# Batch normalisation of 32 x 256 x 128 x 128 floats: two DMA rings, with and without a hold on the stores

## The chip, the cores and the metric

The kernel runs on one core of one Trainium2 chip. The metric is device time in microseconds (us) of one execution; for the kernel before it is the median of three runs. The profile is of one further look at the same program, whose span from the first to the last instruction is a little shorter than the device time of that run (2480.7 us against 2482.53 us).

## The reference

Inference-time batch normalisation in float32: every channel is multiplied by one number and another is added, both worked out from the channel's four parameters.

```python
def reference(x, gamma, beta, running_mean, running_var):
    # x: (32, 256, 128, 128); the others: (256,), reshaped to (1, 256, 1, 1)
    eps = 1e-5
    return gamma * (x - mean) / np.sqrt(var + eps) + beta
```

The input holds 537 MB and the output as much, so the work is nearly all transport: each value is read once, scaled and shifted, and written once.

## The kernel before

A tile is one image and one block of 128 channels: 128 partitions of 16384 floats, 64 KB a partition, 8.39 MB in all. There are 64 tiles and three buffers (`NBUF = 3`), which are used in turn and in place: loaded, computed, stored. SyncE issues all loads, ScalarE all stores, VectorE computes. The semaphores are kept by hand: `loaded[s]` and `stored[s]` count the transfers of buffer `s`, `done` counts VectorE's tiles.

The loads. Tile 0 comes in two parts, so that computing can begin early. A later load waits until its buffer has been stored, and then until the load before it has landed, so that the loads' ring holds one transfer at a time:

```python
nc.sync.dma_start(out=bufs[0][:, left], in_=xr[0][:, left]).then_inc(early, 16)
zeroed = step(nc.vector.memset(rows[:], 0.0))
# ... four small loads of the parameters into rows ...
nc.sync.dma_start(out=bufs[0][:, right], in_=xr[0][:, right]).then_inc(loaded[0], 16)
for i in range(1, NT):
    s, turn = i % NBUF, i // NBUF
    if turn:
        nc.sync.wait_ge(stored[s], 16 * turn)                                  # L99
    inst = nc.sync.dma_start(out=bufs[s][:], in_=xr[i]).then_inc(loaded[s], 16)  # L100
    if i >= 2:
        inst._wait_ge(loaded[(i - 1) % NBUF], 16 * ((i - 1) // NBUF + 1))
```

The early writes. Each of the 16 DMA engines writes 128 bytes of zeros to an output row of tile 0, long before that row is written in earnest:

```python
blanked = step(nc.vector.memset(blank[:], 0.0))
nc.scalar.dma_start(out=outr[0][0 :: P // NE, 0:B], in_=blank[:])._wait_ge(vec, blanked).then_inc(touched, 16)
```

Then the parameters are turned into a scale and a shift per channel (some ten small instructions, left out here), and the tiles follow. A store waits until its tile is computed; ahead of that ScalarE waits until the store before it has landed, so that the stores' ring holds one transfer at a time as well:

```python
def store(i, after):
    s = i % NBUF
    inst = nc.scalar.dma_start(out=outr[i], in_=bufs[s][:]).then_inc(stored[s], 16)   # L143
    inst._wait_ge(done, after)

def turn_of_store(i):
    nc.scalar.wait_ge(stored[(i - 1) % NBUF], 16 * ((i - 1) // NBUF + 1))

compute(0, left)._wait_ge(early, 16)
compute(0, right)._wait_ge(loaded[0], 16)
nc.scalar.wait_ge(touched, 16)
store(0, 2)
for i in range(1, last):
    compute(i)._wait_ge(loaded[i % NBUF], 16 * (i // NBUF + 1))     # L132, on VectorE
    turn_of_store(i)
    store(i, i + 2)
```

`compute` is one VectorE instruction: times `scale_t`, plus `shift_t`. The last tile is shared by VectorE (9216 columns) and ScalarE (7168 columns, L161), and its store waits for both but not for the store before it.

Of the kernel before, what the change touches and what calls it, by code (L numbers as in the profile page):

```python
# [8 lines left out]
NBUF = 3  # L9
# [4 lines left out]
@with_exitstack  # L14
def kernel(
    ctx: ExitStack,
    tc: tile.TileContext,
    x: bass.AP,
    gamma: bass.AP,
    beta: bass.AP,  # L20
    running_mean: bass.AP,
    running_var: bass.AP,
    out: bass.AP,
):
    nc = tc.nc
    eps = 1e-5
    f32 = mybir.dt.float32

    N, C, H, W = x.shape
    P = nc.NUM_PARTITIONS  # L30
    assert C % P == 0
    NCB = C // P
    HW = H * W
    NT = N * NCB
    B = 32
    NQ = P // B
    NE = 16
    NPAR = 4

    xr = x.rearrange("n (cb p) h w -> (n cb) p (h w)", p=P)  # L40
    outr = out.rearrange("n (cb p) h w -> (n cb) p (h w)", p=P)

    params = ctx.enter_context(tc.tile_pool(name="params", bufs=1))
    data = ctx.enter_context(tc.tile_pool(name="data", bufs=1))
    bufs = [data.tile([P, HW], f32, name=f"t{s}", tag=f"t{s}") for s in range(NBUF)]
    rows = params.tile([B, NPAR * C], f32, name="rows", tag="rows")
    turned = params.tile([B, NPAR * C], f32, name="turned", tag="turned")
    par = params.tile([P, NPAR, NCB], f32, name="par", tag="par")
    blank = params.tile([NE, B], f32, name="blank", tag="blank")
    eps_t = params.tile([P, 1], f32, name="eps_t", tag="eps")  # L50
    std_t = params.tile([P, NCB], f32, name="std_t", tag="std")
    rstd_t = params.tile([P, NCB], f32, name="rstd_t", tag="rstd")
    scale_t = params.tile([P, NCB], f32, name="scale_t", tag="scale")
    ms_t = params.tile([P, NCB], f32, name="ms_t", tag="ms")
    shift_t = params.tile([P, NCB], f32, name="shift_t", tag="shift")

    loaded = [tc.alloc_semaphore(f"loaded{s}") for s in range(NBUF)]
    stored = [tc.alloc_semaphore(f"stored{s}") for s in range(NBUF)]  # L60
    touched = tc.alloc_semaphore("touched")
    early = tc.alloc_semaphore("early")
    done = tc.alloc_semaphore("done")
    fetched = tc.alloc_semaphore("fetched")
    vec = tc.alloc_semaphore("vec")
    act = tc.alloc_semaphore("act")

    with tc.tile_critical():  # L68
        count = [0]

        def step(inst, sem=None, value=None):

            if sem is not None:
                inst._wait_ge(sem, value)
            elif count[0]:
                inst._wait_ge(vec, count[0])
            inst.then_inc(vec, 1)
            count[0] += 1
            return count[0]

        left, right = slice(0, HW // 4), slice(HW // 4, HW)
        last = NT - 1

        nc.sync.dma_start(out=bufs[0][:, left], in_=xr[0][:, left]).then_inc(early, 16)
        zeroed = step(nc.vector.memset(rows[:], 0.0))  # L87
        for r, ap in enumerate((running_var, gamma, beta, running_mean)):
            inst = nc.sync.dma_start(out=rows[0:NE, r * C : (r + 1) * C], in_=ap.partition_broadcast(NE))  # L89
            if r == 0:  # L90
                inst._wait_ge(vec, zeroed)
            inst.then_inc(fetched, 16)
# [9 lines that stand above are left out]
                inst._wait_ge(loaded[(i - 1) % NBUF], 16 * ((i - 1) // NBUF + 1))  # L102


        blanked = step(nc.vector.memset(blank[:], 0.0))  # L105
        nc.scalar.dma_start(out=outr[0][0 :: P // NE, 0:B], in_=blank[:])._wait_ge(vec, blanked).then_inc(touched, 16)


        step(nc.vector.memset(eps_t[:], eps))  # L109
        step(nc.vector.transpose(out=turned[:], in_=rows[:]), fetched, 16 * NPAR)  # L110

        blocks = turned.rearrange("p (rc q b) -> p rc q b", q=NQ, b=B)
        flat = par.rearrange("p r cb -> p (r cb)")
        for q in range(NQ):
            placed = step(nc.vector.tensor_copy(out=flat[q * B : (q + 1) * B], in_=blocks[:, :, q, 0]))  # L115
        var_t, gamma_t, beta_t, mean_t = (par[:, r] for r in range(NPAR))
        nc.scalar.activation(  # L117
            out=std_t[:],
            in_=var_t,
            func=mybir.ActivationFunctionType.Sqrt,  # L120
            bias=eps_t[:],
            scale=1.0,
        )._wait_ge(vec, placed).then_inc(act, 1)
        step(nc.vector.reciprocal(out=rstd_t[:], in_=std_t[:]), act, 1)  # L124
        step(nc.vector.tensor_mul(out=scale_t[:], in0=gamma_t, in1=rstd_t[:]))  # L125
        step(nc.vector.tensor_mul(out=ms_t[:], in0=mean_t, in1=scale_t[:]))  # L126
        ready = step(nc.vector.tensor_sub(out=shift_t[:], in0=beta_t, in1=ms_t[:]))  # L127
        nc.vector.wait_ge(vec, ready)

        def compute(i, cols=slice(0, HW)):  # L130
            t, cb = bufs[i % NBUF], i % NCB
            return nc.vector.tensor_scalar(  # L132
                out=t[:, cols],
                in0=t[:, cols],
                scalar1=scale_t[:, cb : cb + 1],
                scalar2=shift_t[:, cb : cb + 1],
                op0=mybir.AluOpType.mult,
                op1=mybir.AluOpType.add,
            ).then_inc(done, 1)

        def store(i, after):
            s = i % NBUF
            inst = nc.scalar.dma_start(out=outr[i], in_=bufs[s][:]).then_inc(stored[s], 16)  # L143
            inst._wait_ge(done, after)

        def turn_of_store(i):
            nc.scalar.wait_ge(stored[(i - 1) % NBUF], 16 * ((i - 1) // NBUF + 1))

        compute(0, left)._wait_ge(early, 16)
        compute(0, right)._wait_ge(loaded[0], 16)  # L150
        nc.scalar.wait_ge(touched, 16)
        store(0, 2)
        for i in range(1, last):
            compute(i)._wait_ge(loaded[i % NBUF], 16 * (i // NBUF + 1))
            turn_of_store(i)
            store(i, i + 2)

        turns = last // NBUF + 1
        compute(last, slice(0, VCOLS))._wait_ge(loaded[last % NBUF], 16 * turns)
        t, cb = bufs[last % NBUF], last % NCB  # L160
        nc.scalar.activation(  # L161
            out=t[:, VCOLS:],
            in_=t[:, VCOLS:],
            func=mybir.ActivationFunctionType.Identity,
            bias=shift_t[:, cb : cb + 1],
            scale=scale_t[:, cb : cb + 1],
        )._wait_ge(loaded[last % NBUF], 16 * turns).then_inc(done, 1)
        store(last, last + 3)

        for s in range(NBUF):  # L170
            nc.sync.wait_ge(stored[s], 16 * ((NT - s + NBUF - 1) // NBUF))
# [30 lines left out]
```

## Time and profile before

| what | value |
|---|---|
| time, median of 3 runs | 2483.66 us (2482.53 to 2484.41) |
| span of the profile | 2480.7 us |
| VectorE busy | 564.1 us, 23% |
| ScalarE busy | 7.9 us |
| bytes by DMA | 1073.84 MB, mean 433 GB/s |
| one tile on VectorE (128x16384) | 8.81 us |
| one load, one store: issue to landing, median | 38.6 us each |

TensorE isn't used. The profile calls the loads' ring q1 and the stores' ring q10. A DMA packet is one contiguous piece that one of the 16 DMA engines moves; here that is a partition's 64 KB. The DMA view gives for each ring its packets, its megabytes and the time that they took as a share of the time of 16 engines in the stretch asked for; packets count where they start, so a share in a short stretch can come out at a little over or under 100%. The waits of SyncE's queue are given by the line of the instruction that waited and by what released it.

### The profile page before, as it was taken

What the parts mean: (1) busy time and instruction counts of PE and PEld (TensorE: products, weight loads), DVE (VectorE), ACT (ScalarE), POOL (GpSimd) and SP (SyncE); (2) the same over time, 40 slices, a digit from 0 to 9 for tenths busy, and PEclk for the clock granted to TensorE, in tenths of its full rate; (3) what the DMA queues carried; (4) which work ended last, traced back from release to release, by engine and by line L of the source; (5) the groups of instructions that cost most, each with busy time, mean ns of one, the idle gap of its engine ahead of it and who ended that gap; (6) DMA issues with size and microseconds to landing.
All of it is one profiled execution on the core that took longest, in us unless ns stands there. A gap on an engine that the chain in (4) does not pass through costs nothing.

```text
span 2480.7 us, 392 instructions
## 1 busy us (share of the span) xinstructions
DVE 564.1 (23%) x77; ACT 7.9 (0%) x3; POOL 0.2 (0%) x4
## 2 busy tenths in 40 slices
DVE  3121221212212122121221222212222122121221
ACT  0000000000000000000000000000000000000001
POOL 0000000000000000000000000000000000000000
DMA  9999999999999999999999999999999999999999
GB/s 415 431 440 433 429 439 435 428 437 439 426 437 440 425 439 439 426 437 438 429 435 437 431 433 437 433 431 437 436 429 436 436 430 434 440 428 434 440 428 406
DMA packets 18739, 1073.84 MB, mean 433 GB/s; under 512 B 2160, under 2 KB 2224, under 8 KB 2224
## 3 DMA queue, kind: packets, MB, share of 16 engines
q1 hardware_dynamic: 9488, 536.94, 50.0%
q10 hardware_dynamic: 9248, 536.88, 49.9%
q14 instruction: 3, 0.02, 0.0%
HBM read 536.94 MB, written 536.87 MB: 433 GB/s over the span
## 4 chain that ended last, share of the span: by engine, by line
DMA 99%; ACT 0%; issue 0%; SPq 0%; DVE 0%; DVEq 0%
DMA t<-in_x_dram 99%; ACT t L161 0%; SPq L89 0%; DVE rows L87 0%; SPq L93 0%; DVE blank L105 0%; DVE eps_t L109 0%; DVEq L197 0%; SPq L68 0%
## 5 line engine op out<-in xcount | busy, mean ns | idle before, releaser
L132 DVE TENSOR_SCALAR t<-t,scale_t,shift_t 128x16384 f32<-128x16384 f32 (+2 forms) x65 | 560.6, 8624 | 1882.4 <-DMA t<-in_x_dram 1882.3
L161 ACT ACTIVATE t<-t,shift_t,scale_t 128x7168 f32<-128x7168 f32 x1 | 6.4, 6361 | 2438.7 <-DMA t<-in_x_dram 2438.7
L110 DVE STREAM_TRANSPOSE turned<-rows 32x1024 f32<-32x1024 f32 x1 | 1.2, 1233 | 7.1 <-DMA rows<-in_running_mean_dram 7.1
L117 ACT ACT_TABLE_LOAD x1 | 1.3, 1283 | 2.7 <-DVE eps_t L109 2.7
L87 DVE MEMSET rows<- 32x1024 f32 x1 | 0.9, 912 | 1.2 <-SPq L68 1.2
L115 DVE COPY par<-turned 32x8 f32<-32x8 f32 x4 | 0.6, 162 | 0.1
L117 ACT ACTIVATE std_t<-par,eps_t 128x2 f32<-128x2 f32 x1 | 0.3, 295 | 7.6 <-DVE par L115 7.6
L124 DVE RECIPROCAL rstd_t<-std_t 128x2 f32<-128x2 f32 x1 | 0.2, 165 | 0.4 <-ACT std_t L117 0.4
L127 DVE TENSOR_TENSOR shift_t<-par,ms_t 128x2 f32<-128x2 f32 x1 | 0.2, 163 | 0.0
L126 DVE TENSOR_TENSOR ms_t<-par,scale_t 128x2 f32<-128x2 f32 x1 | 0.2, 161 | 0.0
L125 DVE TENSOR_TENSOR scale_t<-par,rstd_t 128x2 f32<-128x2 f32 x1 | 0.2, 160 | 0.0
L186 POOL MEMSET const-bfloat16-1.0<- 128x1 bf16 x1 | 0.1, 102 | 0.0
L186 POOL MEMSET const-uint8-127<- 128x1 uint8 x1 | 0.1, 102 | 0.0
L186 POOL MEMSET const-float32-1.0<- 128x1 f32 x1 | 0.1, 99 | 0.0
L105 DVE MEMSET blank<- 16x32 f32 x1 | 0.1, 85 | 0.1
L186 POOL MEMSET const-float32-0.0<- 128x1 f32 x1 | 0.1, 98 | 0.2 <-issue 0.2
L109 DVE MEMSET eps_t<- 128x1 f32 x1 | 0.1, 59 | 0.1
## 6 DMA issues: line engine op xcount, KB each, us to landing
t<-in_x_dram SPq DMA_DIRECT2D x1, 6144.0 KB, 19.4
t<-in_x_dram SPq DMA_DIRECT2D x1, 2048.0 KB, 7.7
out_dram<-t ACTq DMA_DIRECT2D x64, 38.6
t<-in_x_dram SPq DMA_DIRECT2D x63, 38.6
rows<-in_running_var_dram SPq DMA_DIRECT2D x1, 16.0 KB, 6.4
out_dram<-blank ACTq DMA_DIRECT2D x1, 2.0 KB, 5.8
rows<-in_gamma_dram SPq DMA_DIRECT2D x1, 16.0 KB, 6.2
rows<-in_beta_dram SPq DMA_DIRECT2D x1, 16.0 KB, 5.9
```

Source lines behind the costliest of these rows:

```text
L87: zeroed = step(nc.vector.memset(rows[:], 0.0))
L105: blanked = step(nc.vector.memset(blank[:], 0.0))
L110: step(nc.vector.transpose(out=turned[:], in_=rows[:]), fetched, 16 * NPAR)
L115: placed = step(nc.vector.tensor_copy(out=flat[q * B : (q + 1) * B], in_=blocks[:, :, q, 0]))
L117: nc.scalar.activation(out=std_t[:], in_=var_t, func=mybir.ActivationFunctionType.Sqrt, bias=eps_t[:], scale=1.0,)._wait_ge(vec, placed).t ...
L124: step(nc.vector.reciprocal(out=rstd_t[:], in_=std_t[:]), act, 1)
L125: step(nc.vector.tensor_mul(out=scale_t[:], in0=gamma_t, in1=rstd_t[:]))
L126: step(nc.vector.tensor_mul(out=ms_t[:], in0=mean_t, in1=scale_t[:]))
L127: ready = step(nc.vector.tensor_sub(out=shift_t[:], in0=beta_t, in1=ms_t[:]))
L132: return nc.vector.tensor_scalar(out=t[:, cols], in0=t[:, cols], scalar1=scale_t[:, cb : cb + 1], scalar2=shift_t[:, cb : cb + 1], op0=myb ...
L161: nc.scalar.activation(out=t[:, VCOLS:], in_=t[:, VCOLS:], func=mybir.ActivationFunctionType.Identity, bias=shift_t[:, cb : cb + 1], scale ...
L186: nc = _bacc.Bacc("TRN2", target_bir_lowering=False, num_devices=1)
```

## The change

The stores' ring is no longer held to one transfer. ScalarE issues a store as soon as its tile is computed, even while the store before is still under way; the loads' ring alone keeps its hold. The early writes of 128 bytes go too, with their buffer, their memset, their semaphore and the wait for it. The aim is a simpler schedule in which a store that is ready need not wait for another. Loads, buffers, computing and the last tile stay as they were; lines move up, so that L100 and L99 become L98 and L97, L143 becomes L137, and L132 becomes L126.

```diff
--- before.py
+++ after.py
@@ -46,7 +46,6 @@
     rows = params.tile([B, NPAR * C], f32, name="rows", tag="rows")
     turned = params.tile([B, NPAR * C], f32, name="turned", tag="turned")
     par = params.tile([P, NPAR, NCB], f32, name="par", tag="par")
-    blank = params.tile([NE, B], f32, name="blank", tag="blank")
     eps_t = params.tile([P, 1], f32, name="eps_t", tag="eps")
     std_t = params.tile([P, NCB], f32, name="std_t", tag="std")
     rstd_t = params.tile([P, NCB], f32, name="rstd_t", tag="rstd")
@@ -58,7 +57,6 @@
 
     loaded = [tc.alloc_semaphore(f"loaded{s}") for s in range(NBUF)]
     stored = [tc.alloc_semaphore(f"stored{s}") for s in range(NBUF)]
-    touched = tc.alloc_semaphore("touched")
     early = tc.alloc_semaphore("early")
     done = tc.alloc_semaphore("done")
     fetched = tc.alloc_semaphore("fetched")
@@ -102,10 +100,6 @@
                 inst._wait_ge(loaded[(i - 1) % NBUF], 16 * ((i - 1) // NBUF + 1))
 
 
-        blanked = step(nc.vector.memset(blank[:], 0.0))
-        nc.scalar.dma_start(out=outr[0][0 :: P // NE, 0:B], in_=blank[:])._wait_ge(vec, blanked).then_inc(touched, 16)
-
-
         step(nc.vector.memset(eps_t[:], eps))
         step(nc.vector.transpose(out=turned[:], in_=rows[:]), fetched, 16 * NPAR)
 
@@ -143,16 +137,11 @@
             inst = nc.scalar.dma_start(out=outr[i], in_=bufs[s][:]).then_inc(stored[s], 16)
             inst._wait_ge(done, after)
 
-        def turn_of_store(i):
-            nc.scalar.wait_ge(stored[(i - 1) % NBUF], 16 * ((i - 1) // NBUF + 1))
-
         compute(0, left)._wait_ge(early, 16)
         compute(0, right)._wait_ge(loaded[0], 16)
-        nc.scalar.wait_ge(touched, 16)
         store(0, 2)
         for i in range(1, last):
             compute(i)._wait_ge(loaded[i % NBUF], 16 * (i // NBUF + 1))
-            turn_of_store(i)
             store(i, i + 2)
 
         turns = last // NBUF + 1
```

## The prediction

> **What bounds the kernel now.** I read the page's busy times first, then the chain of work that ended last, then the waits of SyncE's DMA queue, then the DMA record cut to short windows. The page gives VectorE 23% of the span and the 16 DMA engines a 9 in every slice. The chain says the same:
>
> ```profile
> DMA 99%; ACT 0%; issue 0%; SPq 0%; DVE 0%; DVEq 0%
> ...
> q1 hardware_dynamic: 9488, 536.94, 50.0%
> q10 hardware_dynamic: 9248, 536.88, 49.9%
> ```
>
> q1 is the ring of the loads (issued by SyncE), q10 the ring of the stores (issued by ScalarE). Their shares of the 16 engines' time add up to 99.9%, so nearly no engine time is unused. One period of the steady part, from one load's issue at 53.02 us to the next at 91.63 us, in the DMA record:
>
> ```profile
> DMA packets 288, 16.78 MB, mean 435 GB/s; under 512 B 32, under 2 KB 32, under 8 KB 32
> q1 hardware_dynamic: 144, 8.39, 50.1%
> q10 hardware_dynamic: 144, 8.39, 50.1%
> ```
>
> Of each ring's 144 packets 128 are rows of 64 KB (a tile has 128 rows of 16384 floats) and 16 are the small ones that count up the semaphore. An engine thus moves 8 + 8 rows in 38.61 us: 2.41 us a row. I call that a slot. A period is 16 slots and holds no empty one.
>
> The two holds are seen in the waits of SyncE's queue:
>
> ```profile
> SPq L100 <- DMA t<-in_x_dram: 1375.3, 62, 48.1
> SPq L99 <- DMA out_dram<-t: 1008.6, 61, 16.7
> ```
>
> L99 ends when the store of three tiles before has landed, 1008.6/61 = 16.5 us after the previous load was issued; L100 ends when the previous load has landed, some 22 us later. So the stores aren't what keeps a load back. L143's issue times agree: ScalarE issues a store about 16.5 to 17 us after the load of its tile landed, though VectorE is done with it after 8.81 us. The remaining 8 us are the wait for the previous store, which the change removes. What do the rings do meanwhile? Cut to the stretch around the end of a load (49.55 to 56.8 us), and around the end of a store (66.4 to 73.7 us), first the one and then the other:
>
> ```profile
> q10 hardware_dynamic: 48, 3.15, 100.1%
> q1 hardware_dynamic: 16, 0.00, 0.1%
> ```
> ```profile
> q1 hardware_dynamic: 48, 3.15, 99.4%
> q10 hardware_dynamic: 16, 0.00, 0.1%
> ```
>
> While the load ring is empty, every engine runs three store rows in a row (48 = 3 x 16) and the load's semaphore packets; while the store ring is empty, three load rows and the store's semaphore packets. Both times the engines are 99 to 100% busy. Elsewhere rows of the two rings alternate. The end of the chain in order of time is the last thing to see:
>
> ```profile
> 2411.84 38.65 DMA t<-in_x_dram
> 2450.50 0.02 issue
> 2450.52 6.36 ACT t L161
> ```
>
> The last load lands at 2450.50, its tile is computed in 6.36 us, and the last store (issued at 2456.91) lands about 22.6 us later, near the end of the span.
>
> **What the Trainium skill says.** "DMA: Bandwidth & Descriptors", section "Queues, rings and completion order", says that a DMA engine takes turns between the rings that have work, a packet at a time. The windows above agree: outside the gaps a load row follows a store row. The same page under "Where 436 GB/s comes from" gives 435.2 GB/s as the ceiling of one core's DMA; this trace moves 434 to 435 in the steady part. Its section "Issuing engines are not separate DMA queues" says that rings of two issuing engines use the same 16 engines and interleave, so that a second ring saves only issue time. The trace agrees: a gap in one ring is filled by the other. That page has nothing on a first write by an engine, which the removed 128-byte writes are for.
>
> **The change part by part.**
>
> (1) The 128-byte writes go, with one memset (85 ns) and ScalarE's wait for them. The page's row for them is
>
> ```profile
> out_dram<-blank ACTq DMA_DIRECT2D x1, 2.0 KB, 5.8
> ```
>
> Issued at 2.30 us they have landed by about 8.1, long before the first store at 30.12, so the wait costs nothing now and its removal gains nothing. Their 2 KB weigh nothing either: 16 packets of 13 ns. What they may do is to take a first-write delay off the first real store. The packet records show that the load row before the first store row is still stretched here, to 2.8 to 3.5 us from 2.41. If more of that comes back without them, I estimate 0 to 1 us (the size of the stretch that is there), on the path, once.
>
> (2) Stores are queued as soon as the tile is computed. In the steady part no slot is empty now, so at most 16 slots a period can stay 16 slots: gain 0 in the 62 periods. What moves is the phase. Call a load's landing T; the next load's first row runs 3.8 us later (landing at 53.0, first row at 56.8). Slot 0 is that row, so T is at slot -1.6. Now the next store is issued at T + 16.5, slot 5.2, and its first row is in slot 7 (73.7 us). After the change it is issued at T + 8.86, slot 2.1; ready some 0.4 slot later (the first load's rows start 1.0 us after its issue) and, as now, one row later than it is ready: slot 4.
>
> At first the stores gain on the loads. When the first store ends (66.4 us), the second is already queued (compute ends at 61.8), so the three load rows in a row become one load row and a store row in turn. The load in flight thereby loses two slots, its landing moves by 2 x 2.41 = 4.8 us, and the store ring comes 8 us forward against it. But a store can't start before its tile is loaded and computed. From there the store ring runs empty ahead of slot 4, and the gap that the hold made is back, made by VectorE's 8.81 us in place of the hold. After one or two periods, going through the slots: loads in 0, 1, 2, 3, 5, 7, 9, 11; stores in 4, 6, 8, 10, 12, 13, 14; the next load in 15, and the eighth store row in the slot after that. The following period needs 17. The average is 16 slots again, 38.6 us. Cost in the steady part: 0.
>
> (3) The end. Store 63 can put its first row on an engine 6.36 us of compute and about 1.0 us of start after the last landing T': T' + 7.4. Now store 62 keeps the engines busy until about T' + 7 to T' + 9 (its semaphore packets run from 2457.4 to 2459.7, and T' is 2450.5), so hardly an engine waits. After the change store 62 is further along: in a period of 15 slots it ends at slot 16, with T' at 13.4, which is T' + 6.2 us; in one of 17 it ends at slot 17 with T' at 15.4: T' + 3.8 us. The 16 engines stand still for 7.4 - 6.2 = 1.2 us or 7.4 - 3.8 = 3.6 us. This is new time, since the bytes are the same.
>
> Sum: 0 to 1 us for (1), 0 for the steady part, 1.2 to 3.6 us for the end: 1.2 to 4.6 us, middle 2.9. I round down to 2.3, because the engines aren't in step (the two groups of semaphore packets at the end are about 1.6 us apart) and stragglers hide part of such a hole: 2483.66 + 2.3 = 2486.0 us.
>
> **The rivals.** (A) The hold is a loss now: the store ring is empty for about 7 us of each period (66.4 to 73.7), and 62 x 7 = 434 us of ring time looks like a prize. Against it: 48 load rows in just that stretch and 99.4% of the engines' time. The change would then be no faster. All that could still be had is the span less the rows: 64 x 2 x 8 rows x 2.418 us (the packet records' duration) = 2476.0 us of the 2480.7, that is 4.7 us, of which 1.9 pass before the first packet and about 1 after the last. At best the change makes 2482.
>
> (B) A second queued store crowds out the load in flight: three store rows to one load row, so that each load takes 2 slots longer, 62 x 4.8 = 298 us, some 2780 us in all. For it: the first such period will do just that. Against it: a store can't run ahead of the load that feeds it, so it can happen in one or two periods only, and the slots given to stores early are missing from their work later.
>
> (C) The hold keeps the 16 engines in step, and without it some run ahead until a load waits for a straggler with empty engines beside it. For it: the groups 1.6 us apart even now, hold and all. Against it: every load still waits for all 16 engines of the one before. If a tenth of a slot were lost per period, 62 x 0.24 = 15 us: 2499 us. I give this about one chance in ten, and half of such cases are small.
>
> **Range and chances.** Low end: nothing at the end and a lucky draw, one or two us under 2483.66: 2482. High end: 4.6 us and a few of (C): 2491. 2% would be 50 us; faster by that is below the rows' 2476 us, and slower needs (B) in every period. Faster 0.003, within 2% 0.99, slower 0.007.
>
> **What would show it.** Right: in the waits of SyncE's queue L98 and L97 (the old L100 and L99) change places in part, the stores having landed about 8 us sooner after each load's issue, so a mean under 12 us in place of 16.5; stores are issued 8.9 us after their load landed; loads take 36 to 41 us in turn with a mean of 38.6; the steady part still has 434 to 435 GB/s; the DMA record has a hole of 1 to 4 us just ahead of the last store. Step (1) is seen in the stretch of rows at 31 to 34 us. Wrong: a steady part under 432 GB/s (then (C)), load periods with a mean above 39 us ((B)), or no hole at the end. If VectorE's 8.81 us per tile became longer beside queued stores, step (2) would also fall.

## The result and the profile after

The changed kernel takes 2506.3 us (2503.28 to 2509.88, 6 runs) against 2483.23 us (6 runs): ratio 1.0089, 95% interval 1.0076 to 1.0102. It is slower by 0.9%, some 23 us, where the prediction had 2486.0 and a range up to 2491.

The span and the rings on the page of the changed kernel:

```profile
span 2504.6 us, 327 instructions
...
q1 hardware_dynamic: 9488, 536.94, 50.4%
q10 hardware_dynamic: 9216, 536.88, 49.5%
```

Multiply the shares by the spans. The loads' ring took 50.0% x 2480.7 = 1240 us of the 16 engines before and 50.4% x 2504.6 = 1262 us after; the stores' ring 49.9% x 2480.7 = 1238 us and 49.5% x 2504.6 = 1240 us. (A share is rounded to 0.1%, so each product is good to 1.2 us.) The shares add up to 99.9% in both. So the DMA engines do not stand idle more; the load packets take 22 us longer for the same bytes, and that is nearly the whole loss of 23.9 us in the span. VectorE is as before, with 564.1 us.

The waits of SyncE's queue:

```profile
SPq L98 <- DMA t<-in_x_dram: 1832.0, 62, 48.2
SPq L97 <- DMA out_dram<-t: 575.1, 61, 16.5
```

On average the store that a load waits for lands 575.1/61 = 9.4 us after the issue of the load before, in place of 16.5: the phase moved forward by 7 us. In the chain in order of time (start, duration, what), loads alternate:

```profile
994.84 37.20 DMA t<-in_x_dram
...
1032.06 41.02 DMA t<-in_x_dram
...
1073.09 36.61 DMA t<-in_x_dram
```

From the load issue at 53.11 us to that at 2435.12 there are 61 periods: 39.05 us each, against 38.67 before (53.00 to 2411.84). The periods account for the loss: 61 x 0.38 = 23 us.

Where in a period? Compare 6.3 us beginning at the issue of a store, which hold the last load rows before the new store's first rows, and these. First the kernel before (1037.55 to 1043.85 us), then the changed one in a short period (1003.7 to 1010.0 us) and in the long one after it (1040.9 to 1047.2 us):

```profile
q1 hardware_dynamic: 26, 1.70, 62.4%
q10 hardware_dynamic: 16, 1.05, 38.4%
```
```profile
q1 hardware_dynamic: 23, 1.51, 63.1%
q10 hardware_dynamic: 15, 0.98, 36.0%
```
```profile
q1 hardware_dynamic: 27, 1.77, 64.8%
q10 hardware_dynamic: 20, 1.05, 38.4%
```

All the load packets here are 64 KB rows, and so are the store packets but for four small semaphore packets in the last window. The mean of a row is the share times 16 engines times 6.3 us, divided by their number: a load row took 0.624 x 100.8 / 26 = 2.42 us before; after the change it took 0.631 x 100.8 / 23 = 2.77 us in the short period and 0.648 x 100.8 / 27 = 2.42 us in the long one. A store row took 2.42 us in all three.

These two periods are a strong and a weak case. The trace has a record of every packet with its start, time and size. Over tiles 3 to 61 the mean of such a window is 2.61 us in short periods and 2.46 us in long ones, and what the load rows of a period take above 2.418 us each adds up to some 0.55 us per engine in a short period and 0.16 us in a long one. Taken over all load rows after 53 us, this excess is 21 us per engine in the changed kernel and 0.5 us before. About 12 of the 21 us sit in load rows that end 9 to 16 us after the load's issue, around the new store's first row; 5 us sit in the rows before those, mostly in a load's first row, and 4 us in the two or three rows after.

### The profile page after: what moved, and what is told of

The parts are those of the page before. It is cut to its first block, busy times and chain, and to the rows that moved or that the text cites. A ratio compares the mean times of both kernels' runs of the same rounds, so it can differ in the third digit from the quotient of the medians.

```text
span 2504.6 us, 327 instructions
## 1 busy us (share of the span) xinstructions
DVE 564.1 (23%) x76; ACT 7.9 (0%) x3; POOL 0.2 (0%) x4
## 3 DMA queue, kind: packets, MB, share of 16 engines
q1 hardware_dynamic: 9488, 536.94, 50.4%
q10 hardware_dynamic: 9216, 536.88, 49.5%
## 4 chain that ended last, share of the span: by engine, by line
DMA 99%; ACT 0%; SPq 0%; issue 0%; DVE 0%; DVEq 0%
DMA t<-in_x_dram 99%; ACT t L150 0%; SPq L87 0%; DVE rows L85 0%; SPq L91 0%; DVE eps_t L103 0%; DVEq L186 0%; SPq L66 0%
## 5 line engine op out<-in xcount | busy, mean ns | idle before, releaser
L126 DVE TENSOR_SCALAR t<-t,scale_t,shift_t 128x16384 f32<-128x16384 f32 (+2 forms) x65 | 560.5, 8624 | 1908.3 <-DMA t<-in_x_dram 1908.2
```

The costliest lines, as they stand in the source:

```text
L126: return nc.vector.tensor_scalar(out=t[:, cols], in0=t[:, cols], scalar1=scale_t[:, cb : cb + 1], scalar2=shift_t[:, cb : cb + 1], op0=myb ...
```

## The experiments

Each kernel ran beside the kernel before on the same chip; ratios are to those runs. Theory P says that what costs is how early in the period the store arrives, W that the missing early writes cost, H that the wait as such keeps the 16 engines in step, I that a ring that stood idle is slow to start. The others are named as they come.

| run | what | store issued after landing of its load | ratio (95%) | us |
|---|---|---|---|---|
| e1 | hold removed, early writes kept | as changed kernel | 1.0094 (1.0077-1.0110) | 2507.5 |
| e2 | hold kept, early writes removed | 16.95 us | 0.9998 (0.9989-1.0007) | 2484.2 |
| f3 | free, computing shared | 6.45 us | 1.0195 (1.0179-1.0210) | 2533.6 |
| changed kernel | free | 8.85 us | 1.0089 (1.0076-1.0102) | 2506.3 |
| e5 | free, 2 dummies | 11.4 us | 1.0043 (1.0028-1.0058) | 2497.2 |
| e6 | free, 4 dummies | 13.9 us | 1.0025 (1.0015-1.0034) | 2493.7 |
| e12 | free, 6 dummies | 16.5 us | 1.0010 (1.0003-1.0017) | 2487.6 |
| e3 | free, 8 dummies | 19.0 us | 1.0009 (1.0000-1.0018) | 2486.4 |
| e7 | free, VectorE delayed | 21.9 us | 1.0012 (1.0005-1.0020) | 2491.0 |
| e8 | free, no computing | as changed kernel | 1.0098 (1.0083-1.0113) | 2511.8 |
| e9 | changed kernel, tiles jump by 32 | as changed kernel | 1.0082 (1.0067-1.0097) | 2504.6 |
| e10 | changed kernel, falling order | as changed kernel | 1.0097 (1.0082-1.0112) | 2508.9 |
| e11 | e2, tiles jump by 32 | as e2 | 1.0002 (0.9993-1.0011) | 2484.2 |
| f1 | both rings free | 8.85 us | 1.0076 (1.0060-1.0092) | 2505.8 |
| f2 | stores held, loads free | see below | 1.2998 (1.2977-1.3020) | 3229.8 |
| e4 | held, 2.5 us pause | see below | 1.0964 (1.0948-1.0981) | 2724.2 |

The kernel before took 2484.59 us beside e1 to e4, 2487.50 beside e5 to e8, 2484.58 beside e9 to e12 and 2485.53 beside f1 to f3.

**Which part of the change? e1 and e2.**

```diff
 e1, from the kernel before:
-            turn_of_store(i)
             store(i, i + 2)
 e2, from the changed kernel:
+            nc.scalar.wait_ge(stored[(i - 1) % NBUF], 16 * ((i - 1) // NBUF + 1))
             store(i, i + 2)
```

> The kernel before with the stores' hold alone removed; the early writes of 128 bytes stay. If the early writes set how the 16 engines stand to one another for the whole run (theory W), this stays near the time before: 2483 to 2487 us. If the free stores are the cause (theories P, H and I below), it is as slow as the changed kernel: 2502 to 2510 us, with loads of 41 and 36.7 us in turn.

> The changed kernel with the stores' hold put back; no early writes. Theory W: about 2500 us or more. All others: the time before, 2481 to 2486 us, with loads of 38.6 us each. What lies between this and the kernel before is the worth of the early writes: I expect 0 to 2 us.

The early writes are worth nothing that can be measured (e2, to 0.1%), and the whole loss comes with the free stores (e1). W falls.

**The wait or the phase? e3 and e4.** In e3 ScalarE is made busy between a tile's computing and its store, with no wait for a store:

```diff
+            if 1 <= i < last:
+                nc.scalar.wait_ge(done, after)
+                for k in range(8):      # each waits for the one before; the last releases the store
+                    nc.scalar.activation(out=rows[:], in_=turned[:], func=Identity, ...)
             inst = nc.scalar.dma_start(out=outr[i], in_=bufs[s][:]).then_inc(stored[s], 16)
```

> The changed kernel (free stores, no early writes), but ScalarE runs eight dummy instructions on a small scratch tile between the end of a tile's computing and the issue of its store (not for the first and last tile). I estimate 8 to 9 us for them, from 6.36 us for 7168 columns, so the store is issued some 17 us after its load landed, as in the kernel before, without any wait for another store. Theory P (what costs is where in the load's 16 slots the store arrives): back to 2482 to 2488 us, all loads near 38.6 us. Theory H (the wait for a landed store keeps the 16 engines in step): stays at 2500 us or more, load rows still stretched.

The eight dummies took 10.15 us, as the timeline of e3 shows (start, duration, engine, line, operation):

```profile
982.60 8.81 DVE L127 TENSOR_SCALAR t<-t,scale_t,shift_t 128x16384 f32<-128x16384 f32 x1 [32.22 <-DMA t<-in_x_dram]
991.45 10.15 ACT L141 ACTIVATE rows<-turned,shift_t,scale_t 32x1024 f32<-32x1024 f32 x8 [30.88 <-DVE t L127]
1001.63 0.34 ACTq L151 DMA_DIRECT2D out_dram<-t  x1
```

The store comes 19.0 us after the landing at 982.6, unheld, and the loss is all but gone. H falls as the cause of the 0.9%: no store waits for another. (What is left, 0.1% here and in e12, isn't explained.) The load rows in the 6.3 us from that store's issue, in e3's DMA record:

```profile
q1 hardware_dynamic: 21, 1.38, 50.6%
```

0.506 x 100.8 / 21 = 2.43 us a load row: not stretched. Yet e3's loads still alternate between 41 and 36.2 us, so the alternation that I predicted is there and costs nothing by itself. And in the short periods, as in this window, the previous store had landed 2.2 us before the new one was issued, with hardly any stretch (0.11 us per engine and period): an idle ring alone isn't enough. In the changed kernel the ring is idle before the store in the short periods too, for 1.6 us, and these have most of the stretch; but f3, below, has the most stretch of these three kernels, and no idle stores' ring. So I falls as the cause, though an idle ring may add to what an early store does; that wasn't tested by itself.

e4 was meant for I alone. It holds the stores and pauses ScalarE (two of the dummies) after the landing of the store before:

```diff
+            nc.scalar.wait_ge(stored[(i - 1) % NBUF], 16 * ((i - 1) // NBUF + 1))
+            # then, as in e3 but with range(2): dummies, then the store
```

> The hold put back, no early writes, and two dummy ScalarE instructions (estimate 2 to 2.3 us) between the landing of the store before and the issue of the next store. The stores' ring is then empty and idle for some 2 us before each store, as the changed kernel has it in every second period (1.97 us). Theory I (a store that meets a ring idle for 2 us stretches the load row before it by about 0.4 us on each engine): 62 x 0.4 = 25 us slower than with the plain hold, near 2508 us. Theories P and H: no more than 0 to 5 us slower than with the plain hold, since phase and step are nearly as before.

No theory foresaw 2724 us, so as a test of I it is inconclusive. A held store that is issued 2.5 us later ends later too, and with the hold this adds up: the stores are issued 19.4, 24.2, 29.4 and 33.9 us after a load's issue in the first four periods. Then loads wait for stores:

```profile
SPq L98 <- DMA out_dram<-t: 2505.6, 61, 50.3
SPq L99 <- DMA t<-in_x_dram: 99.5, 6, 48.0
```

From there both rings run empty together in each period. One such period (1013.47 to 1056.1 us) in e4's DMA record:

```profile
q1 hardware_dynamic: 144, 8.39, 49.4%
q10 hardware_dynamic: 144, 8.39, 45.4%
```

5.2% of the engines' time is unused, and a load row takes 0.494 x 16 x 42.63 / 128 = 2.63 us on the mean. The pause is one that the hold passes on from store to store; it isn't 2.5 us once.

**How much by how much? e5, e6, e12, and f3 on the other side.** e5, e6 and e12 are e3 with `range(2)`, `range(4)` and `range(6)`.

> Free stores, each issued two dummy ScalarE instructions (1.24 us each, measured) after its tile is computed: 11.4 us after its load landed in place of 8.85. If the cost falls off smoothly with the store's place in the load: about 2497 us. If it is a matter of reaching one slot (2.41 us) further: either 2505 or 2487.

> The same with four dummy instructions: the store is issued 13.9 us after the load landed, between the changed kernel (8.85) and the one with eight (19.0). Smooth: about 2490 us. Theory P only asks that it is no slower than with two dummies.

> Free stores, six dummy ScalarE instructions (7.5 us) after each tile's computing: the store is issued 16.4 us after its load landed, within 0.6 us of where the hold puts it (16.9), but waits for no store. Theory P: as the kernel before, ratio 0.999 to 1.002. If the wait as such had a use beyond the phase: 1.003 or more.

The cost falls smoothly. At 16.5 us, where the hold would put it, a free store costs 0.1%. f3 goes the other way and makes computing faster:

```diff
-            compute(i)._wait_ge(loaded[i % NBUF], 16 * (i // NBUF + 1))
+            compute(i, slice(0, VCOLS))._wait_ge(loaded[i % NBUF], 16 * (i // NBUF + 1))
+            # ScalarE: the other 7168 columns, counted on a semaphore of its own
             store(i, i + 2)
```

> The changed kernel with every tile shared by VectorE (9216 columns) and ScalarE (7168 columns, 6.36 us), so that a store is issued about 6.5 us after its load landed in place of 8.85: faster computing. Theory P: slower than the changed kernel, on the line of 1.0025 at 13.9 us, 1.0043 at 11.4 and 1.009 at 8.85: about 1.014, 2515 to 2530 us, with more stretched load rows. If the effect levels off: 2500 to 2510 us. If it was bound to a store at about one slot's place: under 2500 us.

A tile is ready 2.4 us sooner, and the kernel is slower by another 1.1%, more than a straight line would give. The rings of f3, whose span is 2531.6 us:

```profile
q1 hardware_dynamic: 9488, 536.94, 50.9%
q10 hardware_dynamic: 9216, 536.88, 48.9%
```

50.9% x 2531.6 = 1289 us for the loads' ring, 48 us more than before; the stores' ring stays at 1238. Again the load rows alone. Packet records put the excess of load rows over 2.418 us, per engine, at 47.1 us in f3, 21.3 in the changed kernel, 17.6 in e5, 12.2 in e6, 5.9 in e12 and 5.6 in e3. The held e2 has 4.1 us, so e12 and e3 are near it. SyncE's waits show that the stores' ring wasn't idle before a store in f3:

```profile
SPq L98 <- DMA out_dram<-t: 432.5, 61, 16.5
```

The previous store lands 432.5/61 = 7.1 us after a load's issue on average, and the new one was issued at 6.45, before that.

**Is it VectorE? e7 and e8.** In all of these the store that costs also comes directly behind VectorE's work on the tile. e7 delays VectorE and keeps that order; e8 leaves the work out:

```diff
 e7:
+            for k in range(11):                 # each waits for the one before
+                nc.vector.memset(rows[:], 0.0)
             compute(i)._wait_ge(loaded[i % NBUF], 16 * (i // NBUF + 1))
 e8, with seven dummies as in e3:
-            compute(i)._wait_ge(loaded[i % NBUF], 16 * (i // NBUF + 1))
-                nc.scalar.wait_ge(done, after)
+                nc.scalar.wait_ge(loaded[s], 16 * (i // NBUF + 1))
```

> Free stores that are late because VectorE is: it runs eleven dummy memsets of 0.91 us (about 10.7 us with their gaps) before it computes each tile, so the store is issued some 19.5 us after the load landed, but directly behind VectorE, as in the changed kernel. Theory P (the store's place in the load in flight): 2483 to 2489 us, no stretched load rows. Theory V (a load row is slow when a store comes directly behind VectorE's instruction, or VectorE works in the load's last rows before it): near 2505 us, load rows stretched by about 0.35 us per period as in the changed kernel.

> VectorE's work on tiles 1 to 62 is left out (they are stored as loaded); ScalarE waits for the landing, runs seven dummy instructions (8.7 us) and issues the store, which thus comes about 8.8 us after its load landed, as in the changed kernel. Theory P: 2500 to 2508 us, rows stretched as in the changed kernel though VectorE is idle. Theory V: 2483 to 2488 us.

A late store directly behind VectorE (21.9 us after the landing; 19.5 was planned) is as cheap as any late store; an early one with VectorE idle costs what it costs in the changed kernel. V falls.

**Is it the places in memory? e9, e10, e11.**

```diff
+        at = lambda i: (i % 2) * (NT // 2) + i // 2     # e9 and e11; e10: NT - 1 - i
-            inst = nc.sync.dma_start(out=bufs[s][:], in_=xr[i]).then_inc(loaded[s], 16)
+            inst = nc.sync.dma_start(out=bufs[s][:], in_=xr[at(i)]).then_inc(loaded[s], 16)
```

(and likewise for the stores and the choice of scale and shift)

> The changed kernel with the tiles in another order: from one tile to the next the place in memory jumps by 32 tiles (268 MB) there and back, so the rows that a load reads and those that a store writes at the same time lie elsewhere to one another. Theory X (reads are slowed by writes at an unlucky distance in memory): the time moves by more than 8 us from the changed kernel's 1.009 of before. Theory P (only the store's time after its load landed counts): 2500 to 2512 us.

> The changed kernel with the tiles in falling order, so that the load in flight reads the tile below the one that is stored instead of the one above. Theory X: another time than the changed kernel's by more than 8 us. Theory P: 2500 to 2512 us.

> The base for the first of these: the hold put back (no early writes), tiles in the order that jumps by 32. Theory P: 2482 to 2488 us, as with the plain order. Theory X: slower than that by more than 8 us, if the plain order happens to be a lucky one at the held stores' place.

Neither order moves either kernel by more than its interval. Theory X falls for distances of whole tiles; distances within a tile weren't tried.

**Is an early store enough? f1 and f2.** The store's time after landing is the same in f1 as in the changed kernel, but loads are no longer held:

```diff
-            if i >= 2:
-                inst._wait_ge(loaded[(i - 1) % NBUF], 16 * ((i - 1) // NBUF + 1))
```

> Both rings free: a load waits only until its buffer is stored. If the all-store run that the loads' hold makes just ahead of an early store is what slows the load rows after it (theory R), this is faster than the changed kernel: 2482 to 2495 us. If an early store slows the load by its arrival alone (theory P as it stands), or if free loads lose more through empty stretches when a buffer comes free late, 2500 us or more.

f1 takes what the changed kernel takes, but for another reason. Its rings, in a span of 2501.6 us:

```profile
q1 hardware_dynamic: 9488, 536.94, 49.9%
q10 hardware_dynamic: 9216, 536.88, 49.6%
```

49.9% x 2501.6 = 1248 us for the loads' ring: 8 us more than before and not 22; the stores' ring has 1241, 3 us more. The rest, about half of the loss, is at the end, in the last 50.6 us (the engines' busy time, then the clock, the DMA share and GB/s):

```profile
2451.00:2501.60 50.60, 5.08 (x1) 6.36 (x1) 0.00 (x0) 1.00 0.72 310
```

The last load lands at 2470.92, 20 us later than before, when the stores have overtaken it, and the engines are idle for 28% of the last 50.6 us, 14 us, partly while the load's last rows come in and partly while the last tile is computed. (One of its 13 timed runs took 2483.4 us; the others 2500 to 2511.)

Why are f1's load rows hardly stretched? Theory P speaks of the store's place in the load in flight, and here "8.85 us after the landing" isn't that place. A free load is queued behind the one before, and in f1's packet records its first rows run 7.9 us before that one has landed. The store thus arrives 16.7 us after the first rows of the load in flight; in the changed kernel this is 5.1 us, in the kernel before 12.0 and in e3 14.2 (means over tiles 3 to 60). So f1's store is a late one in the load, and its short load rows are what P foresees. Whether a run of store rows alone, made by the loads' hold, takes part (R) isn't shown: f1 removed the run and moved the place at once, and no run varied the length of it by itself. Yet the place isn't all. In the changed kernel it is 6.1 us in short periods, with 0.55 us of excess, and 4.0 us in long ones, with 0.16.

f2 is f1 with the stores' hold of e2:

> Stores held, loads free, no early writes: the counterpart of the changed kernel. If a hold on one ring is enough to keep the two rings' gaps apart: 2482 to 2490 us. If the loads' hold is needed: 2495 us or more.

f2 is far slower than the "2495 us or more" of the second expectation. Its timeline shows load and store issued 0.06 us apart (981.76 and 981.82):

```profile
981.76 102.90 SPq L98 DMA_DIRECT2D t<-in_x_dram  x3
981.82 102.92 ACTq L135 DMA_DIRECT2D out_dram<-t  x3
```

One such period (1032.9 to 1084.5 us) in the DMA record:

```profile
q1 hardware_dynamic: 144, 8.39, 46.2%
q10 hardware_dynamic: 144, 8.39, 40.5%
```

Both rings run empty together, 13% of the engines' time is unused, a load row takes 0.462 x 16 x 51.6 / 128 = 2.98 us, and here store rows are longer too: 0.405 x 16 x 51.6 / 128 = 2.61 us. Over all its load rows a run's mean is 2.42 us in the kernel before, 2.44 in e6, 2.45 in e5, 2.46 in the changed kernel, 2.51 in f3, 2.62 in e4 and 3.04 in f2. This fits one reading: the closer the stores' gap comes to the loads' gap, the longer the load rows take, and where the two fall together (e4, f2) the engines are idle as well.

**A version that beats both** didn't come out of these. e2 is the simplest that equals the kernel before.

## Why the prediction was wrong

- The early writes: right. Nothing to gain or lose that can be measured (e2), and the stretch of the rows before the first store is there with and without them.
- The new phase: right. Stores are issued 8.85 us after their load lands, the mean wait for a landed store is 9.4 us (I had asked for under 12), and loads alternate between short and long periods as the count of slots had it.
- The hole at the end: right in kind and size. The two windows below hold the stretch from the last landing to the last store's issue, before and then after:

```profile
2450.50:2456.90 6.40, 5.08 (x1) 6.36 (x1) 0.00 (x0) 1.00 0.92 399
```
```profile
2476.20:2482.60 6.40, 5.08 (x1) 6.36 (x1) 0.00 (x0) 1.00 0.33 143
```

  The DMA share falls from 0.92 to 0.33. From 2400 us on the packet records show 2.6 us more idle time per engine than before; I had 1.2 to 3.6. It hardly adds to the 23 us of the periods: from the last load's issue to the end of the span the changed kernel takes 69.5 us and the kernel before 68.9, since its stores are further along by then.
- The steady part: wrong, and this is the step that failed: "at most 16 slots a period can stay 16 slots", "Cost in the steady part: 0". The slots were counted rightly, but I took a slot for a constant 2.41 us whatever the order of load and store rows. The trace of the kernel before shows 2.42 us in the phase that its holds set, and I carried that over to a phase that it visits at its first store alone. In the new phase load rows around an early store are stretched (2.61 us on the mean in the windows of short periods, 2.46 in long ones). A period of 17 slots of 2.418 us should take 41.1 us and takes 41.2 on the mean; one of 15 should take 36.3 and takes 36.8. So 61 x 0.38 = 23 us came out of a term put at 0.
- What I took from the Trainium skill, "DMA: Bandwidth & Descriptors", section "Issuing engines are not separate DMA queues", supports the interleaving, and the traces agree. I read into it that the order of the rows is then free of cost. The page doesn't say so, and the runs show otherwise: with the phase alone a load row's mean went from 2.42 us to 2.51 in f3.
- Rival (C) had the right sign and the wrong means: it wanted engines idle beside stragglers. They are 99.9% busy; rows last longer. It was put at 15 us and one chance in ten. Its sign, a steady part under 432 GB/s, is met, from 434 before to 431 (the last number), with the engines' share at 1.00:

```profile
1000.00:2000.00 1000.00, 223.97 (x26) 0.00 (x0) 0.00 (x0) 1.00 1.00 431
```

  Rival (B)'s test, a mean period above 39 us, is met by 0.05 us, but not by its mechanism: the stores do not gain slots in each period.

One window of the kernel before did carry a hint. The load rows just ahead of its very first store took 2.8 to 3.5 us, and that store was issued 6.7 us after the landing at 23.4 us. I put the stretch down to a first write. It is there with the early writes and without, and its size fits an early store (f3, at 6.45 us); that it has the same cause was only argued.

What stays open: why load rows last longer there. Shown is that it comes with a store arriving early in a load while the loads are held, and that it isn't VectorE, the landing wait, an idle ring alone or the tiles' distance in memory. Why the changed kernel's short periods have over three times the stretch of its long ones, at the same 8.85 us, isn't shown either. What in the engines or the memory slows the reads isn't shown by any view here.

## What to carry to other kernels

With two rings on the same DMA engines, a hold isn't only a wait: it sets where in the period each ring runs empty. Keep the two gaps well apart (here stores issued 16 to 22 us after a load's issue were cheap, those of e4, which drifted into the loads' own gap, were not), and measure again after anything that moves them, faster computing included: f3 computed a tile 2.4 us sooner and lost 1.1% more. A full DMA share says that packets are in flight, not that they move at their best rate; multiply share by span for each ring, and divide by the packets, to see which packets grew.

## What the runs showed of the hardware that I had not expected

- Two settings of holds that look alike differ by 29%: loads held and stores free 2506 us, stores held and loads free 3230 us; both held 2484, neither 2506.
- A hold passes a pause on: 2.5 us of pause per store cost 240 us over 62 stores, 3.9 us each, because the pause moved the phase until both rings ran empty together. In the packet records some 103 us of it are longer load rows, and most of the rest is idle time.
- The semaphore packets of a load come one store row after its last data rows: in the kernel before, tile 1's last rows end at 49.6 to 50.2 us and its semaphore packets start at 52.0 to 52.6. This is a part of the loads' gap.
